# RWKV's 64x64 products on four quadrants of the array, with one pool of six PSUM banks

## The chip, the core and the metric

The kernel runs on one core of a Trainium2 chip. The time is the device time of one execution in microseconds, from a median of three runs. The engines are TensorE (PE, with its weight loads shown as PEld), VectorE (DVE), ScalarE (ACT), GpSimd (POOL) and SyncE (SP), which issues most DMAs. Matrix products are written to PSUM, which has eight banks of 128 partitions by 512 fp32 values.

## The reference

Two sequences of 1024 tokens with 1024 channels go through two layers, and then a norm. In each layer the normed input is multiplied with `w_in`, four mixers of 256 channels work on parts of the result, and their gated outputs are multiplied with `w_out` and added to the input.

```python
def _trunk(x, p):
    for l in range(DEPTH):
        zz = _rmsnorm(x, p['norm_g'][l]) @ p['w_in'][l]
        oA = _rwkv_mixer(zz[..., :A_W], ...)          # 4 heads of 64, two directions
        oB = _global_attn_mixer(...)                  # all keys, rotary
        oC = _rglru_mixer(...)
        oD = _window_attn_mixer(...)                  # |t - s| <= 128
        x = x + jnp.concatenate([oA, oB, oC, oD], -1) @ p['w_out'][l]
    return _rmsnorm(x, p['final_g'])

def step(S, inp):                                     # of mixer A, one token, both directions
    rt, wt, kt, vt, kkt, at = inp
    sk = jnp.einsum('bhij,bhj->bhi', S, kkt)
    S = S * wt[:, :, None, :] - sk[..., None] * (kkt * at)[:, :, None, :] + vt[..., None] * kt[:, :, None, :]
    return S, jnp.einsum('bhij,bhj->bhi', S, rt)
```

## The kernel before, in words

The work is cut into units, one for each layer and sequence. A front (`front`) norms a unit's input, makes the projections (`proj_store`, `proj_gate`, each 128 channels by 1024 tokens, three passes over high and low parts, in two tiles `pj` of PSUM), and runs mixers A and C. `mixer_bd` is attention for one or two units, `out_proj` and `out_last` the output projections. `ORDER` on line 38 gives the order in the program: F0 F1 B0 O0 F2 B1 O1 F3 B23 O23.

The program is written with tiles from pools. A planner lays down the order of each engine's instructions when the program is built: it goes through a simulated time, and on each engine takes the instruction that stands first in the program among those whose inputs are ready and for whose tile a buffer is free. On the chip each engine then follows that fixed order. So the projections of a front, which are written behind mixer A, and attention, which is written behind the next front or ahead of it, fill the time in which mixer A waits.

Mixer A (`mixer_a`) takes a pair of heads at a time, one on partitions 0-63 and one on 64-127, and half of the tokens, 8 chunks of 64: four blocks per front, 16 in all. For each block:

- `a_early` loads and shifts the inputs and normalizes the keys. `a_decay` makes the decays of a direction: two products `pl` of 512 columns, one from rows 0-63 of `up` and `wa` and one from rows 64-127, each followed by an activation that reads it.
- `a_prep_dir`, for each direction, multiplies the decayed keys `bk` and queries `ar` of each chunk and head: `pg` (192 columns, two chunks to a bank), then `pk` and `pn` (128 columns, four chunks to a bank). VectorE masks one part of each tile into `nl`, `kt`, `na`, and ScalarE copies the other.
- `tok` transposes the values of each chunk and head with the identity (64 columns, one bank, one ScalarE copy).
- `a_inverse` inverts the masked products by VectorE and by products of 32x32.
- `a_post`, for each direction and four chunks: `pf` (128 columns), a ScalarE copy into `xq`, then two `pw` (128 columns), each subtracted by VectorE from what it corrects. Then `pz` and `py`, products of 64 columns with the values.
- After two blocks `a_steps` runs the state through 16 chunks, one small product and one VectorE addition per step.

All these products are 64 by 64. In a bank the head on partitions 0-63 is computed from rows 0-63 of the array into its columns 0-63, the other head from rows 64-127 into columns 64-127, so two of the array's four quadrants are used. Both operands of a product lie on the partitions of its rows, and its result goes to the PSUM partitions of its columns.

PSUM's eight banks are divided by pools (lines 60 to 63): two for `pj`, three for `px` (attention's scores, rope, norms, transposes of the input and the output), two for `pa` (mixer A and the gates of mixer C), one for `ps` (`a_steps`, `a_out`).

Of the kernel before, what the change touches and what calls it, by code (L numbers as in the profile page):

```python
# [12 lines left out]
ALU = mybir.AluOpType  # L13
# [5 lines left out]
T = 1024  # L19
# [7 lines left out]
HC = NCH // 2  # L27
A_OFF, B_OFF, C_OFF, D_OFF = 0, 1152, 1920, 2432
# [23 lines left out]
class Trunk:  # L52
    def __init__(self, ctx, tc, w):
# [7 lines left out]
        self.pxp = pool("px", 3, space=PSUM)  # L61
        self.pap = pool("pa", 2, space=PSUM)
        self.psp = pool("ps", 1, space=PSUM)
# [3 lines left out]
    # ---- allocation helpers  # L67
# [33 lines left out]
    # ---- constants  # L101
# [39 lines left out]
    def load_layer(self, l):  # L141
# [39 lines left out]
        # softplus(-lam) = max(-lam, 0) + log1p(exp(-|lam|)), log1p(e) = 2 atanh(e / (2 + e))  # L181
# [28 lines left out]
    # ---- y = 1 / sqrt(x), x > 0, on small tiles  # L210
# [13 lines left out]
    # ---- 1/rms of each token, from the sums of squares over each partition's channels  # L224
# [20 lines left out]
    def x_first(self, pool, xs, xdram, st, hpool=None, L=None):  # L245
        """input tokens: 1/rms, channel-major to DRAM, normed if hpool is given"""
# [28 lines left out]
    def norm_rows(self, pool, st, half, ps):  # L275
        """st along the tokens, in every partition"""
# [74 lines left out]
    def proj_gate(self, pool, wsrc, c0, h, dst):  # L351
        """2 silu(gate), channel-major"""
# [52 lines left out]
        # unit keys  # L405
# [19 lines left out]
    def a_late(self, pool, keep, bd, L, P):  # L425
# [4 lines left out]
        # values, token-major by head, in place of the state's queries  # L430
# [5 lines left out]
        # bonus  # L436
# [6 lines left out]
    def a_decay(self, pool, d, L, P):  # L443
# [27 lines left out]
    def a_prep_dir(self, pool, keep, d, L, P):  # L471
        """decayed queries and keys of one direction, their products within the chunks, token-major forms"""
        nc = self.nc
        ch = lambda t: t.rearrange("p (c t) -> p c t", t=CH)
        H = [slice(0, 64), slice(64, 128)]
# [771 lines left out]
```

## Time and profile before

| what | value |
|---|---|
| time, median of three runs | 3475.95 us (3475.06 to 3481.63) |
| span of the profiled execution, first to last instruction | 3466.1 us |
| its own time | not given beyond the span; the median lies 9.85 us above the span |
| PE busy | 3180.8 us, 27314 products |
| DVE, ACT, POOL busy | 1931.1, 1283.9, 1160.0 us |
| mean granted clock of TensorE | 0.948 |

The busy time of an engine is the time in which at least one of its instructions runs; products that overlap count once. An fp32 product of the code appears in the profile as two products with two weight loads. A granted clock of 1.00 is 2.4 GHz, and 0.5 is 1.2 GHz.

### The profile page before, as it was taken

To read this page: it belongs to the slowest core of one execution; us is meant where nothing else is said; L and a number is where in the kernel's file an instruction comes from. 1 tells how busy PE (TensorE), PEld (TensorE's weight loads), DVE (VectorE), ACT (ScalarE), POOL (GpSimd) and SP (SyncE) were. 2 spreads that over 40 slices of the span, in tenths; PEclk is the share of its full clock that TensorE was granted. 3 is DMA by queue.
4 is the path that set the end of the run, shared out by engine and by line. 5 is a ranking of instruction groups with operands and counts; after the bars stand their busy time and mean duration, and the time that the engine had idled before them with its cause. 6 is when DMAs were issued, how large, how long until landed. Compare 5 with 4: busy or idle time off the path is not lost. (4 is left out here: it accounts for less than half of the span.)

```text
span 3466.1 us, 67345 instructions
## 1 busy us (share of the span) xinstructions
PE 3180.8 (92%) x27314; PEld 2253.7 (65%) x27314; DVE 1931.1 (56%) x3849; ACT 1283.9 (37%) x2397; POOL 1160.0 (33%) x1008
## 2 busy tenths in 40 slices
PE   6999999999779798999988989999999898898797
PEld 5777777777445476777666457777777554554486
DVE  6254434352886626423677957433663887679523
ACT  5332223222744423222544433324423434437322
POOL 2233232232432334222343333421333333434443
PEclk9999999999879899999989989999999898999799
DMA  7332333232220333323241124322333211111753
GB/s 247 107 109 83 92 115 92 91 90 91 91 76 16 114 117 127 89 80 94 90 149 51 39 80 145 120 85 83 125 112 99 63 38 54 49 46 38 260 190 133
DMA packets 382270, 343.99 MB, mean 99 GB/s; under 512 B 125708, under 2 KB 264968, under 8 KB 381960
## 3 DMA queue, kind: packets, MB, share of 16 engines
q1 hardware_dynamic: 242568, 270.48, 24.2%
q10 hardware_dynamic: 139392, 69.22, 7.1%
q8 instruction: 214, 3.51, 0.4%
q14 instruction: 96, 0.79, 0.1%
HBM read 217.84 MB, written 121.63 MB: 98 GB/s over the span
## 5 line engine op out<-in xcount | busy, mean ns | idle before, releaser
L99 PE MATMUL pj<-h,wh 128*128 128x512 f32 x3200 | 1063.3, 410 | 24.6 <-ACT h L234 11.1
L99 PEld LDWEIGHTS pj<-h,wh 128*128 128x128 f32 x3200 | 597.1, 190 | 213.0 <-issue 36.0
L324 POOL TENSOR_TENSOR wl<-wr,wh 128x512 fp32r<-128x512 f32 x264 | 354.1, 1341 | 1013.8 <-ACT wh L323 912.0
L99 PE MATMUL pj<-h,wl 128*128 128x512 f32 x1600 | 644.0, 407 | 1.9 <-POOL wl L324 1.9
L967 POOL TENSOR_TENSOR ac<-e,ac 128x512 f32<-128x512 f32 (+3 forms) x192 | 226.2, 1184 | 470.3 <-ACT e L954 309.0
L99 PE MATMUL pj<-oh,wh 128*128 128x512 f32 x1024 | 342.5, 414 | 34.0 <-ACT oh L234 23.9
L99 PE MATMUL px<-b,b 128*128 128x512 f32 (+6 forms) x1072 | 348.7, 415 | 27.0 <-DVE mxd L914 9.6
L99 PEld LDWEIGHTS pj<-h,wl 128*128 128x128 f32 x1600 | 304.2, 190 | 89.4 <-issue 19.9
L323 ACT CAST wh<-wr 128x512 fp32r<-128x512 f32 x264 | 163.2, 618 | 526.9 <-PE pj L99 517.1
L99 PEld LDWEIGHTS px<-b,b 128*128 128x128 f32 (+1 forms) x1072 | 191.0, 200 | 208.8 <-issue 139.9
L954 ACT ACTIVATE e<-px 128x512 f32<-128x512 f32 (+3 forms) x384 | 191.1, 516 | 246.2 <-PE px L99 238.6
L99 PEld LDWEIGHTS pj<-oh,wh 128*128 128x128 f32 x1024 | 195.9, 195 | 95.4 <-ACT oh L234 32.4
L99 PE MATMUL pa<-ar,bk 64*64 64x128 f32 (+1 forms) x2048 | 195.4, 314 | 27.2 <-ACT nl L507 13.7
L99 PE MATMUL pj<-oh,wl 128*128 128x512 f32 x512 | 204.5, 405 | 1.7 <-POOL wl L324 1.7
L97 PE MATMUL pj<-e,v 128*64 128x512 f32 (+3 forms) x768 | 186.9, 561 | 9.8 <-ACT e L954 9.5
L99 PEld LDWEIGHTS pa<-ar,bk 64*64 64x64 f32 x2048 | 132.3, 138 | 79.4 <-issue 37.5
L967 DVE TENSOR_TENSOR ac<-e,ac 128x512 f32<-128x512 f32 (+3 forms) x192 | 149.0, 780 | 54.3 <-ACT e L954 41.4
L626 DVE TENSOR_TENSOR kt<-kt,pa 128x512 f32<-128x512 f32 x64 | 43.8, 684 | 196.9 <-PE pa L99 196.7
L346 ACT ACTIVATE m<-pj 128x512 f32<-128x512 f32 x136 | 80.8, 594 | 134.2 <-PE pj L99 126.0
L99 PE MATMUL pa<-nl,bk 64*64 64x128 f32 x2048 | 126.3, 273 | 2.5 <-ACT bk L619 2.5
L99 PEld LDWEIGHTS pa<-nl,bk 64*64 64x64 f32 x2048 | 110.8, 133 | 26.0 <-issue 17.2
L902 DVE TENSOR_REDUCE mxb<-px 128x1 f32<-128x512 f32 x160 | 107.7, 682 | 35.5 <-PE px L99 34.9
(285 smaller groups left out, 5132.1 us busy)
## 6 DMA issues: line engine op xcount, KB each, us to landing
wr<-in_w_in_dram ACTq DMA_DIRECT2D x200, 256.0 KB
zd<-m SPq DMA_DIRECT2D x136, 256.0 KB
tg<-og SPq DMA_DIRECT2D x64, 512.0 KB
rw<-zd SPq DMA_DIRECT2D x192, 128.0 KB
og<-m SPq DMA_DIRECT2D x64, 256.0 KB
wr<-in_w_out_dram ACTq DMA_DIRECT2D x64, 256.0 KB
xo<-xd SPq DMA_DIRECT2D x64, 256.0 KB
halo<-zd SPq DMA_DIRECT2D x56, 256.5 KB
```

What stands on the lines that cost most here:

```text
L97: return self.nc.tensor.matmul(out=out, lhsT=lhsT, rhs=rhs, start=start, stop=stop, skip_group_check=True)
L99: self.nc.tensor.matmul(out=out, lhsT=lhsT, rhs=rhs, start=start, stop=stop)
L323: nc.scalar.copy(out=hi, in_=raw)
L324: nc.gpsimd.tensor_tensor(out=lo, in0=raw, in1=hi.bitcast(F32), op=ALU.subtract)
L346: self.nc.scalar.mul(out=m, in_=p, mul=scale)
L626: nc.vector.tensor_tensor(out=fl(dst), in0=fl(dst), in1=fl(pw), op=ALU.subtract)
L902: nc.vector.tensor_reduce(out=mx[:, i, half:half + 1], in_=p, axis=AX.X, op=ALU.max)
L954: last = nc.scalar.activation(out=e[:, :n], in_=p[:, :n], func=AF.Exp)
L967: (nc.gpsimd if (x + r) % ADDM else nc.vector).tensor_tensor(out=acc[r][:, os], in0=es[r][:, :n], in1=acc[r][:, os], op=ALU.add)
```

## The change

The three pools `px`, `pa` and `ps` become one pool of six banks, from which `px()`, `pa()` and `pss()` all take. `pj` keeps its two.

In mixer A the products of 64x64 outside `a_inverse`, `a_steps` and `a_out` are set out anew, over all four pairs of a row half and a column half (`QUADS`), in turn. Chunks 0-3 of a block go to one column half and chunks 4-7 to the other, and each of the two row halves has a bank of its own, so that the products of four (head, chunk) pairs follow each other with four different quadrants. The layout of `nl`, `kt`, `na`, `xq` follows: the index that was the chunk group is now the head, and the partition half is now the chunk group. In `a_post` the four quadrants carry the data back, so that `ar`, the state and `y` lie as before. The 192-column products of the second head are split in 64 and 128 columns, on different column halves. `tok` and `y` are copied by ScalarE in two pieces, since they now lie in two banks. In `a_decay` both tiles are taken and both products issued before the two activations. Comments are removed throughout.

```diff
+HS = (slice(0, 64), slice(64, 128))
+QUADS = ((0, 0), (1, 1), (1, 0), (0, 1))
-        self.pxp = pool("px", 3, space=PSUM)
-        self.pap = pool("pa", 2, space=PSUM)
-        self.psp = pool("ps", 1, space=PSUM)
+        self.pxp = pool("px", 6, space=PSUM)
...
     def pa(self, shape=(128, 512)):
-        return self.t(self.pap, "pa", shape)
+        return self.t(self.pxp, "px", shape)
     def pss(self, shape=(128, 512)):
-        return self.t(self.psp, "ps", shape)
+        return self.t(self.pxp, "px", shape)
...
     def tok(self, dst, src):
-        p = self.pa((128, HC, CH))
-        for j in range(HC):
-            for hs in (slice(0, 64), slice(64, 128)):
-                self.mm(p[hs, j], src(j)[hs], self.ident[hs, hs])
-        self.nc.scalar.copy(out=dst, in_=p)
+        ps = [self.pa((128, 4, CH)) for _ in range(2)]
+        for j in range(4):
+            for q, h in QUADS:
+                self.mm(ps[h][HS[q], j], src(4 * q + j)[HS[h]], self.ident[HS[h], HS[h]])
+        for h in range(2):
+            self.nc.scalar.copy(out=dst[:, 4 * h:4 * h + 4], in_=ps[h])
...
     def a_decay(...):
-        for (b0, dst, bias) in ((0, th, X_HW0), (64, tau, X_HA0)):
-            pl = self.pa()
-            self.mm(pl, L["up"][b0:b0 + 64, d, 128 * p:128 * p + 128], wa[b0:b0 + 64])
+        pls = [self.pa() for _ in range(2)]
+        for i in range(2):
+            self.mm(pls[i], L["up"][HS[i], d, 128 * p:128 * p + 128], wa[HS[i]])
+        for (pl, dst, bias) in ((pls[0], th, X_HW0), (pls[1], tau, X_HA0)):
             nc.scalar.activation(out=dst, in_=pl, func=AF.Tanh, scale=0.5, bias=...)
...
     def a_prep_dir(...):
-        for j0 in range(0, HC, 2):
-            pg = self.pa((128, 2, 3, CH))
+        for j0 in range(0, 4, 2):
+            pg = [self.pa((128, 2, 3, CH)) for _ in range(2)]
             for j in range(2):
-                for hs in H:
-                    self.mm(pg[hs, j], bk[hs, j0 + j], ar[hs, j0 + j])
+                c = [4 * q + j0 + j for q in range(2)]
+                self.mm(pg[0][HS[0], j], bk[HS[0], c[0]], ar[HS[0], c[0]])
+                self.mm(pg[1][HS[1], j, 0], bk[HS[1], c[1]], ar[HS[1], c[1], 0])
+                self.mm(pg[0][HS[1], j], bk[HS[0], c[1]], ar[HS[0], c[1]])
+                self.mm(pg[1][HS[0], j, 0], bk[HS[1], c[0]], ar[HS[1], c[0], 0])
+                self.mm(pg[1][HS[1], j, 1:3], bk[HS[1], c[0]], ar[HS[1], c[0], 1:3])
+                self.mm(pg[1][HS[0], j, 1:3], bk[HS[1], c[1]], ar[HS[1], c[1], 1:3])
...
-        for g in range(2):
-            pk, pn = self.pa((128, 4, 2, CH)), self.pa((128, 4, 2, CH))
-            for j in range(4):
-                c = 4 * g + j
-                for hs in H:
-                    self.mm(pk[hs, j], bk[hs, HC + c], ar[hs, c, 1:3])
-                    self.mm(pn[hs, j], ar[hs, c, 0], bk[hs, HC + c:2 * HC + 1:HC - c])
+        pk = [self.pa((128, 4, 2, CH)) for _ in range(2)]
+        for j in range(4):
+            for q, h in QUADS:
+                c = 4 * q + j
+                self.mm(pk[h][HS[q], j], bk[HS[h], HC + c], ar[HS[h], c, 1:3])
...
+        pn = [self.pa((128, 4, 2, CH)) for _ in range(2)]
+        for j in range(4):
+            for q, h in QUADS:
+                c = 4 * q + j
+                self.mm(pn[h][HS[q], j], ar[HS[h], c, 0], bk[HS[h], HC + c:2 * HC + 1:HC - c])
...
     def a_post(...):
-            for g in range(2):
-                pf = self.pa((128, 4, 2, CH))
-                for j in range(4):
-                    for hs in H:
-                        self.mm(pf[hs, j], nl[hs, 4 * g + j, 0], na[hs, j])
-                nc.scalar.copy(out=xq, in_=pf)
-                for (i, dst) in ((0, kt), (1, ar[:, 4 * g:4 * g + 4, 1:3])):
-                    pw = self.pa((128, 4, 2, CH))
-                    for j in range(4):
-                        for hs in H:
-                            self.mm(pw[hs, j], xq[hs, j, i], nl[hs, 4 * g + j, 1:3])
-                    nc.vector.tensor_tensor(out=fl(dst), in0=fl(dst), in1=fl(pw), op=ALU.subtract)
+            pf = [self.pa((128, 4, 2, CH)) for _ in range(2)]
+            for j in range(4):
+                for q, h in QUADS:
+                    self.mm(pf[h][HS[q ^ h], j], nl[HS[q], 4 * h + j, 0], na[h][HS[q], j])
+            for h in range(2):
+                nc.scalar.copy(out=xq[h], in_=pf[h])
+            pw = [self.pa((128, 4, 2, CH)) for _ in range(2)]
+            for j in range(4):
+                for q, h in QUADS:
+                    s = HS[q ^ h]
+                    self.mm(pw[h][HS[q], j], xq[h][s, j, 0], nl[s, 4 * h + j, 1:3])
+            for h in range(2):
+                nc.vector.tensor_tensor(out=fl(kt[h]), in0=fl(kt[h]), in1=fl(pw[h]), op=ALU.subtract)
...
+        pz = [self.pa((128, 2, 4, CH)) for _ in range(2)]
+        for d in range(2):
+            for j in range(4):
+                for q, h in QUADS:
+                    self.mm(pz[q][HS[h], d, j], P["kt", d, h][HS[q], j, 1], vt[HS[q], 4 * h + j])
...
+        for q in range(2):
+            nc.scalar.copy(out=y[:, 4 * q:4 * q + 4], in_=py[q])
```

The second `pw` (onto `ar`) and `py` are set out in the same way. The number of products stays, but for `pg`: 24 instead of 16 per direction and block.

## Rows read from the trace of the kernel before

**Rows 1.** The page: busy us of each engine (share of the span), x instructions
```profile
PE 3180.8 (92%) x27314; PEld 2253.7 (65%) x27314; DVE 1931.1 (56%) x3849; ACT 1283.9 (37%) x2397; POOL 1160.0 (33%) x1008
```
**Rows 2.** Table by windows, A beside projections: length, busy us, PEclk, DMA share, GB/s
```profile
480.00:840.00 360.00, 360.00 (x3162) 276.62 (x3161) 129.40 (x321) 92.64 (x181) 100.02 (x85) 1.00 0.29 87
...
sum 1645.00, PE 1621.09 PEld 1232.70 DVE 697.54 ACT 513.78 POOL 501.18; mean PE 270.18 PEld 205.45 DVE 116.26 ACT 85.63 POOL 83.53
```
**Rows 3.** Table by windows, A beside attention (PE, PEld, DVE, ACT, POOL)
```profile
880.00:1160.00 280.00, 243.31 (x1965) 136.96 (x1963) 225.31 (x404) 142.87 (x269) 104.72 (x99) 0.87 0.17 52
...
sum 1040.00, PE 926.10 PEld 549.46 DVE 837.34 ACT 501.76 POOL 390.31; mean PE 308.70 PEld 183.15 DVE 279.11 ACT 167.25 POOL 130.10
```
**Rows 4.** Same windows, instructions on tile pa alone: projections' six, attention's three
```profile
sum 1645.00, PE 375.53 PEld 272.85 DVE 123.95 ACT 124.84; mean PE 62.59 PEld 45.47 DVE 20.66 ACT 20.81
...
sum 1040.00, PE 297.03 PEld 211.75 DVE 89.54 ACT 93.63; mean PE 99.01 PEld 70.58 DVE 29.85 ACT 31.21
```
**Rows 5.** Timeline of PE, 64x64 runs: start us, length us, engine, line, operation, tiles
```profile
254.08 1.09 PE L99 MATMUL pa<-na,nl 64*64 64x128 f32 x16
255.10 0.50 PE L99 MATMUL pj<-h,wh 128*128 128x512 f32 x1
...
300.46 2.08 PE L99 MATMUL pa<-ar,kt 64*64 64x64 f32 x64
...
542.91 0.87 PE L99 MATMUL pa<-ar,bk 64*64 64x192 f32 x8
...
560.64 1.15 PE L99 MATMUL pa<-ident,v 64*64 64x64 f32 x32
...
577.55 1.52 PE L99 MATMUL pa<-ar,bk 64*64 64x192 f32 x16
...
652.14 1.96 PE L99 MATMUL pa<-nl,bk 64*64 64x128 f32 x32
```
**Rows 6.** Timeline of PE and PEld: products of 512 columns of other shapes
```profile
561.72 1.12 PE L99 MATMUL pa<-wa,up 64*128 64x512 f32 x2
...
867.41 1.98 PE L99 MATMUL pa<-cxc,gw 128*128 128x512 f32 x4
...
1048.97 0.20 PEld L97 LDWEIGHTS pj<-e,v 128*64 128x64 f32 x4 [0.25 <-ACT e L954]
1048.97 1.08 PE L97 MATMUL pj<-e,v 128*64 128x512 f32 x4
```
**Rows 7.** Groups by form, PE: xcount | busy us, mean ns | idle us before, releasers
```profile
L99 PE MATMUL pa<-ar,bk 64*64 64x192 f32 x1024 | 108.9, 346 | 13.1 <-ACT nl L507 6.1 <-DVE bk L490 3.9 <-ACT z L638 2.7
...
L99 PE MATMUL pa<-ar,bk 64*64 64x128 f32 x1024 | 87.4, 282 | 14.1 <-ACT nl L507 7.6 <-ACT kt L520 6.4
...
L99 PE MATMUL pa<-wa,up 64*128 64x512 f32 x128 | 76.9, 690 | 6.0 <-DVE kk L421 3.1 <-ACT na L522 2.9
...
L99 PE MATMUL pa<-cxc,gw 128*128 128x512 f32 x128 | 68.9, 646 | 6.2 <-ACT ctg L764 5.3 <-issue 0.8
```
**Rows 8.** Groups: score products of attention, and what reads them
```profile
L99 PE MATMUL px<-b,b 128*128 128x512 f32 (+6 forms) x1072 | 348.7, 415 | 27.0 <-DVE mxd L914 9.6
...
L954 ACT ACTIVATE e<-px 128x512 f32<-128x512 f32 (+3 forms) x384 | 191.1, 516 | 246.2 <-PE px L99 238.6 <-DVE ac L967 2.2 <-PE pj L99 1.8
...
L902 DVE TENSOR_REDUCE mxb<-px 128x1 f32<-128x512 f32 x160 | 107.7, 682 | 35.5 <-PE px L99 34.9
...
L914 DVE TENSOR_REDUCE mxd<-px 128x1 f32<-128x384 f32 (+1 forms) x80 | 41.2, 523 | 17.8 <-PE px L99 17.3
```
**Rows 9.** Timeline, tiles pk and pn of one group: first products, last copy
```profile
549.16 0.43 PE L99 MATMUL pa<-ar,bk 64*64 64x128 f32 x4
...
551.91 0.37 ACT L522 COPY na<-pa 128x256 f32<-128x256 f32 x1
```
**Rows 10.** Timeline of ACT: the copy of a pf into xq
```profile
646.91 0.59 ACT L619 COPY bk<-pa 128x512 f32<-128x512 f32 x1 [6.38 <-PE pa L99]
```
**Rows 11.** Instructions on tile pa, all engines, in 40 slices of the span
```profile
busy tenths in 40 slices 0899999999499997999999999999399999993000
```

More of the change, by code (lines that the diff above doesn't have):

```diff
@@ L499, in a_prep_dir @@
         P["nl", d] = nl
-        for j0 in range(0, HC, 2):
-            pg = self.pa((128, 2, 3, CH))
+        for j0 in range(0, 4, 2):
+            pg = [self.pa((128, 2, 3, CH)) for _ in range(2)]
             for j in range(2):
-                for hs in H:
-                    self.mm(pg[hs, j], bk[hs, j0 + j], ar[hs, j0 + j])
-            nc.vector.tensor_tensor(out=fl(nl[:, j0:j0 + 2, 0:2]), in0=fl(pg[:, :, 0:2]), in1=m(d, 0, 2, 2),
-                                    op=ALU.mult)
-            nc.scalar.copy(out=nl[:, j0:j0 + 2, 2], in_=pg[:, :, 2])
@@ new lines, in a_prep_dir @@
+                self.mm(pg[0][HS[0], j], bk[HS[0], c[0]], ar[HS[0], c[0]])
[5 more added lines that the diff above has]
+            for h in range(2):
+                n = slice(4 * h + j0, 4 * h + j0 + 2)
+                nc.vector.tensor_tensor(out=fl(nl[:, n, 0:2]), in0=fl(pg[h][:, :, 0:2]), in1=m(d, 0, 2, 2), op=ALU.mult)
+                nc.scalar.copy(out=nl[:, n, 2], in_=pg[h][:, :, 2])
@@ new lines, in a_prep_dir @@
+        for h in range(2):
+            P["kt", d, h] = self.t(pool, f"kt{d}{h}", (128, 4, 2, CH))
+            P["na", d, h] = self.t(pool, f"na{d}{h}", (128, 4, 2, CH))
+        pk = [self.pa((128, 4, 2, CH)) for _ in range(2)]
[3 more added lines that the diff above has]
+                self.mm(pk[h][HS[q], j], bk[HS[h], HC + c], ar[HS[h], c, 1:3])
+        for h in range(2):
+            kt = P["kt", d, h]
+            nc.vector.tensor_tensor(out=kt[:, :, 0], in0=pk[h][:, :, 0], in1=m(d, 1, 4), op=ALU.mult)
+            nc.scalar.copy(out=kt[:, :, 1], in_=pk[h][:, :, 1])
@@ L523, in a_prep_dir @@
+        pn = [self.pa((128, 4, 2, CH)) for _ in range(2)]
[3 more added lines that the diff above has]
+                self.mm(pn[h][HS[q], j], ar[HS[h], c, 0], bk[HS[h], HC + c:2 * HC + 1:HC - c])
+        for h in range(2):
+            na = P["na", d, h]
+            nc.vector.tensor_tensor(out=na[:, :, 0], in0=pn[h][:, :, 0], in1=m(1 - d, 0, 4), op=ALU.mult)
+            nc.scalar.copy(out=na[:, :, 1], in_=pn[h][:, :, 1])
         return kd
@@ L606, in a_post @@
         nc = self.nc
-        H = [slice(0, 64), slice(64, 128)]
+        fl = lambda t: t.rearrange("p n x t -> p n (x t)")
         for d in range(2):
@@ new lines, in a_post @@
+            na, kt = [[P[n, d, h] for h in range(2)] for n in ("na", "kt")]
+            pf = [self.pa((128, 4, 2, CH)) for _ in range(2)]
+            for j in range(4):
+                for q, h in QUADS:
+                    self.mm(pf[h][HS[q ^ h], j], nl[HS[q], 4 * h + j, 0], na[h][HS[q], j])
+            for h in range(2):
+                nc.scalar.copy(out=xq[h], in_=pf[h])
[4 more added lines that the diff above has]
+                    self.mm(pw[h][HS[q], j], xq[h][s, j, 0], nl[s, 4 * h + j, 1:3])
@@ new lines, in a_post @@
+            for h in range(2):
+                nc.vector.tensor_tensor(out=fl(kt[h]), in0=fl(kt[h]), in1=fl(pw[h]), op=ALU.subtract)
+            pw = [self.pa((128, 4, 2, CH)) for _ in range(2)]
+            for j in range(4):
+                for q, h in QUADS:
+                    s = HS[q ^ h]
+                    self.mm(pw[q][HS[h], j], xq[h][s, j, 1], nl[s, 4 * h + j, 1:3])
+            for q in range(2):
+                am = ar[:, 4 * q:4 * q + 4, 1:3]
+                nc.vector.tensor_tensor(out=fl(am), in0=fl(am), in1=fl(pw[q]), op=ALU.subtract)
@@ L627, in a_post @@
         vt = P["vt"]
+        pz = [self.pa((128, 2, 4, CH)) for _ in range(2)]
         for d in range(2):
-            pz = self.pa((128, HC, CH))
-            for c in range(HC):
-                for hs in H:
-                    self.mm(pz[hs, c], P["kt", d, c // 4][hs, c % 4, 1], vt[hs, c])
-            for g in range(2):
-                c0 = HC * hf + 4 * g
-                if d == 0:
-                    nc.scalar.copy(out=S["z"][c0 // 4][:, :, 0], in_=pz[:, 4 * g:4 * g + 4])
-                else:
-                    nc.scalar.copy(out=S["z"][(12 - c0) // 4][:, ::-1, 1], in_=pz[:, 4 * g:4 * g + 4])
@@ L639, in a_post @@
-        py = self.pa((128, HC, CH))
+            for j in range(4):
+                for q, h in QUADS:
+                    self.mm(pz[q][HS[h], d, j], P["kt", d, h][HS[q], j, 1], vt[HS[q], 4 * h + j])
+        for q in range(2):
+            c0 = HC * hf + 4 * q
+            nc.scalar.copy(out=S["z"][c0 // 4][:, :, 0], in_=pz[q][:, 0])
+            nc.scalar.copy(out=S["z"][(12 - c0) // 4][:, ::-1, 1], in_=pz[q][:, 1])
+        py = [self.pa((128, 4, CH)) for _ in range(2)]
         for d in range(2):
-            for c in range(HC):
-                for hs in H:
-                    self.mm(py[hs, c], P["kt", d, c // 4][hs, c % 4, 0], vt[hs, c], start=d == 0 and c == 0,
-                            stop=d == 1, skip=True)
+            for j in range(4):
+                for q, h in QUADS:
+                    self.mm(py[q][HS[h], j], P["kt", d, h][HS[q], j, 0], vt[HS[q], 4 * h + j],
+                            start=d == 0 and j == 0, stop=d == 1, skip=True)
@@ L645, in a_post @@
         y = P["ar", 1][:, :, 0]
-        nc.scalar.copy(out=y, in_=py)
+        for q in range(2):
+            nc.scalar.copy(out=y[:, 4 * q:4 * q + 4], in_=py[q])
         S["y", hf] = y
```

12 lines of the change are left out of this document (1 added, 11 removed).

## The prediction

> **What bounds the kernel now.** I read the page's busy table first [rows 1]: TensorE is busy 3180.8 us of 3466.1 (92%), VectorE 56%, ScalarE 37%, so no other engine comes near over the whole run. Such a share hides stages, and the table by windows came next. In six windows where mixer A runs beside the projections, TensorE is busy 1621 of 1645 us, at a granted clock of 1.00 in the one shown, and VectorE only 698 [rows 2]. There every microsecond taken off TensorE comes off the path, because the next projection stands right behind in its queue. In three windows where mixer A runs beside attention, TensorE is busy 926 of 1040 us, at a clock of 0.87 in the one shown, and VectorE 837 [rows 3]: two engines near their limit, and TensorE time is worth less. Instructions on the tile `pa`, nearly all of them mixer A's, hold 375.5 us of TensorE in the six windows and 297.0 in the three [rows 4]: 56% and 44%.
>
> Then the question how fast 64x64 products run today. One product in the code is two records (the 8 products of one `pf` are 16 records). Two timeline runs of one shape and different length give the pace without their ends: 16 more records cost 1.96 - 1.09 = 0.87 us at 128 columns, 32 more cost 2.08 - 1.15 = 0.93 at 64 columns, 8 more cost 1.52 - 0.87 = 0.65 at 192 [rows 5]. Per two records that is 109, 58 and 163 ns. The two records are the two heads': the code puts them on the diagonal of the array, (rows 0-63, columns 0-63) and (rows 64-127, columns 64-127).
>
> **The quadrants.** Each of 16 blocks (4 fronts, 4 half pairs) has, by the code, 32 products of 192 columns, 160 of 128 (per direction 16 each in `pk`, `pn`, `pf`, 32 in `pw`) and 80 of 64 (16 in `tok`, 32 each in `pz`, `py`). A pair of products takes two pair steps, so there are as many steps as products: 32 x 163 + 160 x 109 + 80 x 58 = 27.3 us per block, 437 us in all. After the change four products stand in four quadrants. For 128 and 64 columns that halves the steps. The 192-column products of the second head are split in 64 + 128: a group of four costs its longest quadrant, 2 x (58 + 109) = 334 ns, eight groups per block, 2.7 us for 5.2. After: 2.7 + 8.7 + 2.3 = 13.7 us per block. Saved: 13.6 x 16 = 218 us.
>
> Do four run at once? The value products of two heads share all 128 rows and differ in columns: four records of 512 columns take 1.08 us, while four of `gw`, each on the whole array and so one by one, take 1.98 [rows 6]. So two column halves fed from the same rows run side by side, as the two row halves do above. What no row shows is two row halves writing the same 64 PSUM partitions at once, as (0,0) and (1,0) now do, each in a bank of its own. Bounds: 0 to 218. I take 90%, 196 us, since a quad falls back to pairs where the planner finds the second of its two banks taken.
>
> The four weight loads of those value products are over within 0.20 us, while the products on the same rows go on to 1.08 [rows 6]. The Trainium skill (TensorE: Matmul & The Clock Gate, "Part 3: Packing small matmuls") says that a weight load overlaps running matmuls only where its row group differs, which speaks against two quadrants on the same rows; the rows above differ from it, and it stays as a rival.
>
> **The decays.** `a_decay` made two products of 512 columns with an activation between them; now both are issued together, and they sit on the two row halves. One takes 1.12 us; side by side two should take what the value pair takes, 1.08 us [rows 6]. 32 x (2 x 1.12 - 1.08) = 37 us. Bounds 0 (the planner still puts projections between) to 37.
>
> **Changes of shape.** A run of 16 records holds the engine from 254.08 to 255.10, 1.02 us for 8 steps of 0.109 [rows 5]: 0.15 us per run to get in and out of 64x64. Per direction and block the runs go from 10 to 12 (4 `pg`, 2 `pk` with `pn`, 2 `pf`, 2 to 4 `pw`) to 7. 32 x 3 to 5 x 0.15 = 14 to 24 us. Since broken quads make new runs I take 12; bounds 0 to 24.
>
> **The banks.** Mixer A (with C's gates) had two banks, its state steps one, attention and rope three; now all share six. TensorE's idle time just ahead of the four costliest waits on `pa` is 39 us (13.1 + 14.1 + 6.0 + 6.2) [rows 7], ahead of the score products on `px` 27 us [rows 8]. All of it gone would be 66 us; I take a third, 22. Downwards: a score tile may now wait for a bank in A's hands. There are 624 score tiles on `px` (384 + 160 + 80) [rows 8]; the length of one eviction, 0.37 us [rows 9], for each would be -231 us. The value lies near the idle rows, as A's bursts are short: the two tiles of `pk` and `pn` are made and read within 3.1 us (549.16 to 552.28) [rows 9].
>
> **What else moves.** VectorE's evictions keep number and size. ScalarE copies `tok` and `y` in two pieces: 32 more copies, 2 x 0.37 [rows 9] for 0.59 us [rows 10], 5 us on an engine busy 37%, hidden behind projections, and 5 us if not. No DMA is added or moved, so SP's and POOL's queues keep their order but for the planner's new timing. The one wait added is on the first product that writes a quad's second bank: behind it in TensorE's order stand that quad's other products and whatever the planner put next, and VectorE and ScalarE wait for those with their evictions.
>
> **The sum.** In the six windows a saved microsecond counts full, in the three attention windows I count 0.6 (between 0, if VectorE takes over, and 1; TensorE at 89% is nearer to the upper end): 0.56 + 0.44 x 0.6 = 0.82. Quadrants 196 x 0.82 = 162, decays 37 x 0.82 = 30, shapes 12, banks 22: 226 us. Span 3466.1 - 226 = 3240. The median of the runs shown is 3475.95, 9.85 above the span of the one profiled; no other time of that execution is given, so I add 9.85: 3250 us, 6.5% faster. Its own range is 3210 to 3300.
>
> **Rivals.**
> 1. VectorE takes over beside attention, and nothing of the 44% is gained. For: 837 of 1040 us busy there, and the granted clock, already 0.87, would fall further where TensorE idles more [rows 3]. Against: TensorE's 89% in the same rows. 0.56 x (196 + 37) + 12 = 142, banks nothing: 3334 us.
> 2. A's chain was the spine. `pa` has work in nearly every slice [rows 11], and between a ScalarE copy that ends at 647.50 [rows 10] and the products that read it, at 652.14 [rows 5], lie 4.6 us. With six banks the planner can close such gaps, and A's next unit starts earlier. Against: TensorE is full beside the projections anyway. All of quadrants, decays, shapes and idle rows: 196 + 37 + 24 + 66 = 323, 3153 us.
> 3. Two row halves on the same PSUM partitions take turns, so quads are no faster than pairs. 30 + 12 + 22 = 64: 3412 us.
> 4. Weight loads wait for products on the same rows. A 128-column step of four then takes 109 + 58 = 167 for 218, a 64-column one 116 for 116 (no gain), a group of 192 columns 334 + 4 x 58 = 566 for 650 (27% of its saving). 47% of the 140 us of 128 columns plus 27% of 40: 77, x 0.9 x 0.82 = 57, and 64: 121, 3355 us.
> 5. Slower: the score tiles starve. Attention loses its three own banks to A's bursts of two to six. It decides from 226 / 624 = 0.36 us of wait per score tile; at 0.5 us, 312 us, the time is 3562 us. For: ScalarE already waits 238.6 us for score products [rows 8]. Against: six banks stand where three were, and A's are free again in about 3 us.
>
> **How the numbers follow.** Forecast 0.50, rival 1 0.17, 2 0.12, 3 0.08, 4 0.07, 5 0.06. The range 3140 to 3400 holds the forecast and rivals 1, 2 and 4, about 0.83 with their tails. Only rival 5 is slower, and a mild form of it could end within 0.2%, about the least that a measurement here can tell from no change: faster 0.92, same 0.03, slower 0.05.
>
> **What would show it.** Right: four records start close together and the next four 109 ns later at 128 columns, so that the 16 records of a `pf` that took 1.09 us take about 0.6; TensorE's busy time near 2950 us at a share of about 91%; the two products of `a_decay` as one run of four records. Wrong: fours that go as two pairs 109 ns apart (rivals 3 and 4, by where the weight loads start); attention windows as long as before with VectorE above 85% (rival 1); ScalarE's wait for score products well above 238.6 us (rival 5). A time under 3200 or above 3300 would mean that a term above is mis-sized by more than its working allows.

## The result and the profile after

The changed kernel takes 3852.58 us (median of 4 runs) beside 3475.51 for the kernel before: ratio 1.1078, 95% interval 1.1062 to 1.1094. The forecast was 3250, the range 3140 to 3400. It is 10.8% slower, and the direction was wrong.

The page of the kernel after: busy us and share of each engine; TensorE's busy tenths in 40 slices; the granted clock, likewise.
```profile
PE 3045.1 (79%) x27826; PEld 2201.8 (57%) x27826; DVE 1912.3 (50%) x3849; ACT 1284.9 (33%) x2429; POOL 1141.9 (30%) x1008
...
PE   7999844899965487999997448798989744788998
...
PEclk9999865899975688989997668898999855889999
```
TensorE is busy 136 us less than in [rows 1], and its share falls from 92% to 79%. The slices show four holes (44, 54, 44, 44) that the kernel before does not have, and the granted clock falls in each. Mean clock and span of the kernel after:
```profile
core 0: 3851.1 us, clock 0.852
```
Between the two levels 2.4 and 1.2 GHz, 0.852 means (1 - 0.852) x 2 x 3851 = 1140 us at the lower one; before, at a mean of 0.948, it was 360 us of 3466.

The table by windows of the kernel after names the holes (length; busy us of PE, PEld, DVE, ACT, POOL; clock; DMA share; GB/s). First, mixer A beside projections:
```profile
710.00:1110.00 400.00, 372.65 (x3987) 289.01 (x3988) 172.91 (x397) 127.76 (x258) 97.74 (x95) 0.96 0.31 92
...
sum 1510.00, PE 1402.98 PEld 1087.46 DVE 662.11 ACT 475.98 POOL 363.20; mean PE 350.74 PEld 271.87 DVE 165.53 ACT 119.00 POOL 90.80
```
Second, A's end, C and rope with no projections beside them, a kind of stretch that did not exist before:
```profile
1110.00:1320.00 210.00, 107.79 (x1805) 81.64 (x1805) 103.61 (x242) 61.12 (x99) 37.47 (x33) 0.62 0.11 33
...
sum 880.00, PE 451.33 PEld 340.32 DVE 432.37 ACT 254.82 POOL 160.85; mean PE 112.83 PEld 85.08 DVE 108.09 ACT 63.70 POOL 40.21
```
Third, attention, now without A:
```profile
1330.00:1510.00 180.00, 156.82 (x640) 86.61 (x640) 127.73 (x196) 81.48 (x165) 83.74 (x71) 0.89 0.15 47
...
sum 725.00, PE 619.02 PEld 338.53 DVE 534.63 ACT 332.27 POOL 345.67; mean PE 206.34 PEld 112.84 DVE 178.21 ACT 110.76 POOL 115.22
```
In the 880 us of the second kind no engine is busy more than 51%, and the clock is 0.62 in the one shown. Before, those stages lay beside projections and attention [rows 2, 3].

The products did get faster. The timeline of PE after (start us, length us, records):
```profile
404.50 1.12 PE L99 MATMUL px<-bk,ar 64*64 64x128 f32 x32
...
406.03 1.13 PE L99 MATMUL px<-wa,up 64*128 64x512 f32 x4
...
467.36 1.99 PE L99 MATMUL px<-na,nl 64*64 64x128 f32 x32 [0.75 <-DVE nl L620]
```
Against [rows 5], 32 records of 128 columns take 1.12 us for 1.96: four quadrants run side by side, two row halves onto the same PSUM partitions among them. Against [rows 6], four decay records take 1.13 us, where two took 1.12. The third row shows the clock eating the gain: in a hole, at 1.2 GHz (granted clock 0.50 from 467 to 470 us), a quad run of 32 takes 1.99 us, as long as the pairs took before.

What grew is waiting. Instructions on rope's tile `rp`, by windows, of the kernel before and then after:
```profile
170.00:400.00 230.00, 15.85 (x84) 11.52 (x84) 8.24 (x12) 3.79 (x6) 22.85 (x18) 1.00 0.33 99
...
570.00:710.00 140.00, 6.24 (x36) 4.73 (x36) 2.75 (x4) 2.52 (x4) 7.25 (x6) 1.00 0.29 88
```
```profile
170.00:400.00 230.00, 0.00 (x0) 0.00 (x0) 0.00 (x0) 1.27 (x2) 0.00 (x0) 0.98 0.29 84
400.00:570.00 170.00, 0.00 (x0) 0.00 (x0) 0.00 (x0) 0.00 (x0) 0.00 (x0) 0.74 0.19 50
570.00:710.00 140.00, 28.81 (x84) 18.67 (x84) 23.56 (x28) 3.69 (x6) 23.33 (x18) 0.61 0.21 70
```
Before the change all 84 products of the front's six ropes had run by 400 us. After it two of rope's activations had run by 400 us, so its input was there, and not one product until 570. The timeline of PE after shows what they stood behind:
```profile
573.69 3.78 PE L99 MATMUL px<-ident,ar 64*64 64x64 f32 x64 [6.73 <-DVE gnt L219]
577.39 1.86 PE L99 MATMUL px<-bones,rp 128*128 128x2 f32 x8
```
The first row is the last products of mixer A (`a_out`), the second rope's first, right behind them. TensorE had sat idle for 6.73 us, until VectorE released A's products, and ran no product of rope in that time.

And the next front stood behind rope. Instructions on `rp`, first of the kernel before, then of the kernel after: kind, count, shortest/median/longest ns, first and last start.
```profile
L99 PE MATMUL px<-bones,rp x192: 165/251/272, 202.7 to 2566.1; 128*128 128x2 f32 x192
...
L305 DVE SCALAR_TENSOR_TENSOR m<-m,par,rp x48: 733/748/1893, 443.4 to 2253.4; 128x512 f32<-128x512 f32 x48
```
```profile
L99 PE MATMUL px<-bones,rp x192: 209/352/374, 577.4 to 3238.8; 128*128 128x2 f32 x192
...
L305 DVE SCALAR_TENSOR_TENSOR m<-m,par,rp x48: 739/751/1771, 682.2 to 2637.5; 128x512 f32<-128x512 f32 x48
```
L305 is the norm that opens the next front, at 682.2 us for 443.4. Its first step, a ScalarE copy into `rp` at 678.9, waits 11.5 us for rope's last addition on GpSimd: by the code, rope works in the front's SBUF space, which the next front takes over. So behind the first front there was no next projection to fill TensorE for some 240 us. In the other three holes it is attention that comes late: its first products on `px` start at 1337.5 us, after the second hole, and at 879.3 before the change.

The theory that the runs test: **a pool gives its banks out in the order of the program, so in one shared pool a tile written later in the program waits until every earlier one has its bank.** Rope, C's gates and attention are all written behind mixer A. (The planner, as described ahead of the prediction, takes any ready instruction "for whose tile a buffer is free"; by the theory a bank is free only for the tile whose turn it is.) The rival: six banks for all are too few, whatever the order. The expectations below name two more: quads need two banks at once and lose them to others ("starving"), and the quadrants' products spoil the planned order ("planner").

### The profile page after: what moved, and what is told of

It is laid out like the page before. It is cut to its first block, busy times and chain, and to the rows that moved or that the text cites. A ratio compares the mean times of both kernels' runs of the same rounds, so it can differ in the third digit from the quotient of the medians.

```text
span 3851.1 us, 68791 instructions
## 1 busy us (share of the span) xinstructions
PE 3045.1 (79%) x27826; PEld 2201.8 (57%) x27826; DVE 1912.3 (50%) x3849; ACT 1284.9 (33%) x2429; POOL 1141.9 (30%) x1008
## 5 line engine op out<-in xcount | busy, mean ns | idle before, releaser
L99 PE MATMUL px<-b,b 128*128 128x512 f32 (+6 forms) x1072 | 319.4, 405 | 1.1 <-ACT e L980 0.6
L99 PEld LDWEIGHTS px<-b,b 128*128 128x128 f32 (+1 forms) x1072 | 206.8, 208 | 124.5 <-issue 88.7
L993 DVE TENSOR_TENSOR ac<-e,ac 128x512 f32<-128x512 f32 (+3 forms) x192 | 180.3, 955 | 63.1 <-POOL ac L993 33.0
L1079 DVE TENSOR_TENSOR xo<-xo,pj 128x512 f32<-128x512 f32 x64 | 44.0, 687 | 218.8 <-PE pj L99 218.7
L833 PE MATMUL px<-ident,rp 128*128 128x128 f32 x96 | 26.8, 434 | 130.0 <-POOL rp L828 130.0
L687 DVE TENSOR_TENSOR z<-z,px 128x128 f32<-128x128 f32 x112 | 32.0, 285 | 195.0 <-PE px L99 195.0
L99 PE MATMUL px<-ar,bk 64*64 64x128 f32 (+2 forms) x2560 | 99.9, 295 | 34.2 <-DVE bk L495 31.9
L645 DVE TENSOR_TENSOR kt<-kt,px 128x512 f32<-128x512 f32 x64 | 41.9, 685 | 171.0 <-PE px L99 171.0
L99 PE MATMUL pj<-b,b 128*128 128x512 f32 (+1 forms) x144 | 69.6, 483 | 69.9 <-DVE mxb L928 33.2
L99 PE MATMUL px<-bk,nl 32*32 32x16 f32 (+1 forms) x3072 | 42.3, 197 | 93.6 <-ACT bk L577 81.4
```

Of the source, the lines that this page charges most:

```text
L99: self.nc.tensor.matmul(out=out, lhsT=lhsT, rhs=rhs, start=start, stop=stop)
L645: nc.vector.tensor_tensor(out=fl(kt[h]), in0=fl(kt[h]), in1=fl(pw[h]), op=ALU.subtract)
L687: nc.vector.tensor_tensor(out=z(i), in0=z(i), in1=zp, op=ALU.add)
L833: nc.tensor.transpose(out=pb[:, 128 * i:128 * i + 128], in_=ex[:, 128 * i:128 * i + 128], identity=self.ident)
L993: (nc.gpsimd if (x + r) % ADDM else nc.vector).tensor_tensor(out=acc[r][:, os], in0=es[r][:, :n], in1=acc[r][:, os], op=ALU.add)
L1079: nc.vector.tensor_tensor(out=xo, in0=xo, in1=p, op=ALU.add)
```

## The experiments

All ratios are to the kernel before, with 95% intervals. In the diffs `+` is the experiment; `-` is the changed kernel, or the kernel before where the text says so.

**The two halves of the change apart.** Quadrants with the old pools:
```
-        self.pxp = pool("px", 6, space=PSUM)
+        self.pxp = pool("px", 3, space=PSUM)
+        self.pap = pool("pa", 2, space=PSUM)
+        self.psp = pool("ps", 1, space=PSUM)
...
-        return self.t(self.pxp, "px", shape)
+        return self.t(self.pap, "pa", shape)
...
-        return self.t(self.pxp, "px", shape)
+        return self.t(self.psp, "ps", shape)
```


> The changed kernel with the three pools of before put back (px 3 banks, pa 2, ps 1). Order theory (a pool hands its banks out in the order in which the program asks, so in one pool everything written behind mixer A waits until A took its last bank): the loss is gone and the quadrants' gain stays, 3200 to 3300 us; the first rope product runs beside mixer A again, at about 250 us into the span, not after 580. Starving theory (quads need two banks at once and lose them to others): with two banks for A it gets worse, over 3500. Planner theory (the quadrants' products themselves spoil the planned order): still 3700 to 3900.

Measured 3410.97 us, 0.9801 (0.9770 to 0.9831). The loss is gone, which the starving and the planner theory do not allow, but the time lies 111 us above the range of the order theory. And the kernel before, with nothing but the one pool:
```
-        self.pxp = pool("px", 3, space=PSUM)
-        self.pap = pool("pa", 2, space=PSUM)
-        self.psp = pool("ps", 1, space=PSUM)
+        self.pxp = pool("px", 6, space=PSUM)
...
-        return self.t(self.pap, "pa", shape)
+        return self.t(self.pxp, "px", shape)
...
-        return self.t(self.psp, "ps", shape)
+        return self.t(self.pxp, "px", shape)
```


> The kernel before with nothing changed but its three pools merged into one of six banks. Order theory: slower than the changed kernel or near it, 3900 to 4050 us, with rope after mixer A and TensorE idle for some 700 us or more. Starving theory: 3450 to 3550, since pairs of products need one bank at a time. Planner theory: 3475 plus or minus 40.

Measured 4069.91 us, 1.1697 (1.1663 to 1.1732). So the pool alone costs 4070 - 3476 = 594 us, and the rest of the change gives 4070 - 3853 = 217 on top of it, 65 with the old pools. The whole loss is the pool's; the starving and planner theories, which expected at most 3550 here, fall.

**Two pools instead of one or three** (`px` 3; `pa`, `ps` and the gates share 3):
```
-        self.pxp = pool("px", 6, space=PSUM)
+        self.pxp = pool("px", 3, space=PSUM)
+        self.pap = pool("pa", 3, space=PSUM)
...
-        return self.t(self.pxp, "px", shape)
+        return self.t(self.pap, "pa", shape)
...
-        return self.t(self.pxp, "px", shape)
+        return self.t(self.pap, "pa", shape)
```


> The changed kernel with two pools: px 3 banks, and one of three for mixer A's blocks, its state steps and C's gates. Order theory: rope and attention are free of A, 3250 to 3400 us; C's gates and the next pair's blocks still stand behind A's state steps, so it is slower than with three pools. Starving theory: like three pools or better, as A has three banks for two. Planner theory: 3700 to 3900.

Measured 3444.18 us, 0.9917 (0.9887 to 0.9947), 44 us above the range. Sharing among instructions that are all mixer A's and C's costs 33 us beside the three pools: fewer pools alone are not the trouble.

**One late tile in attention's pool.** The kernel before, where only the state steps move into `px`, which gets their bank:
```
-        self.pxp = pool("px", 3, space=PSUM)
+        self.pxp = pool("px", 4, space=PSUM)
...
-        self.psp = pool("ps", 1, space=PSUM)
...
-        return self.t(self.psp, "ps", shape)
+        return self.t(self.pxp, "px", shape)
```


> The kernel before, without quadrants; only the one bank of the state steps (ps) joins px, which then has four; pa keeps its two. Order theory: that alone is enough, since rope and attention now stand behind the state steps that end mixer A: 3850 to 4100 us, first rope product after the first unit's last step (above 900 us if A goes at its old pace, 600 if A runs alone). Shortage theory: faster or same, 3430 to 3480, as no one has fewer banks.

Measured 4112.56 us, 1.1834 (1.1816 to 1.1853), the slowest of all and 13 us above the range. Instructions on `rp` of that kernel:
```profile
L98 PE MATMUL px<-bones,rp x192: 209/352/372, 676.6 to 3494.7; 128*128 128x2 f32 x192
...
L304 DVE SCALAR_TENSOR_TENSOR m<-m,par,rp x48: 737/751/1768, 745.4 to 2828.0; 128x512 f32<-128x512 f32 x48
```
Mixer A kept its two banks, and no bank was lost to anyone. But the state steps, A's last work, now stand ahead of rope in `px`, and rope begins at 676.6 instead of 202.7, the norm at 745.4 instead of 443.4.

**Rope out of the shared pool** (the changed kernel, `px` 5, one bank for rope):
```
-        self.pxp = pool("px", 6, space=PSUM)
+        self.pxp = pool("px", 5, space=PSUM)
+        self.prp = pool("pr", 1, space=PSUM)
...
-        pst = self.px((128, 4, 2))
+        pst = self.pr((128, 4, 2))
...
-        pb = self.px()
+        pb = self.pr()
...
-        pp = self.px()
+        pp = self.pr()
```


> The changed kernel, but rope's three tiles per step come from a pool of their own of one bank, and the shared pool has five. Order theory: rope runs beside mixer A again (from about 250 us), so the front's input is free early and the next front's norm and projections start before mixer A ends, at 400 to 550 us instead of 682; C's gates and attention still stand behind A. Between the changed kernel and three pools: 3550 to 3750 us. If a shortage of banks were the cause: no better than 3850, as A and attention have one bank less.

Measured 3629.48 us, 1.0454 (1.0430 to 1.0477). Rope's products begin at 211.9 us, the time drops by 223 with one bank less in the pool, and what is left is attention. Instructions on its tile `b` in three windows:
```profile
940.00:980.00 40.00, 4.00 (x7) 2.14 (x7) 2.76 (x4) 9.56 (x16) 12.35 (x10) 0.75 0.49 146
980.00:1200.00 220.00, 0.00 (x0) 0.00 (x0) 0.00 (x0) 0.00 (x0) 0.00 (x0) 0.65 0.12 30
1200.00:1390.00 190.00, 90.84 (x297) 56.90 (x297) 6.78 (x4) 18.61 (x32) 12.12 (x10) 0.87 0.09 31
```
Its inputs are there and 7 products run, all into the projections' tile `pj`; then none for 220 us, while the next front's A and C finish (A's last output at 1173 us, C's scans from 1189), and then all, from 1208 us.

**C's gates moved.** Quadrants with the three old pools, the gates from `px` instead of `pa` (two lines against that version):
```
-                            pg = self.pa()
+                            pg = self.px()
```


> Three pools as before, the quadrants, and the gates of mixer C taken from px instead of pa. Order theory: in pa the gates stand behind the whole of A, in px they don't, so mixer C's scans come out while A still runs (before the last state steps of A); time 3180 to 3290, at or under quads with three pools. Starving theory: no difference to three pools beyond 1%. Planner theory: 3700 to 3900.

Measured 3856.03 us, 1.1084 (1.1054 to 1.1113): a miss, 566 us above the range, and as slow as the whole change. (It lies in the range of the planner theory, which the 3411 us with the same quadrants had excluded.) I had not asked what is written behind the gates in `px`. C's SBUF space lies over mixer A's, so the gates come after A's blocks (the last products that read `xq` end at 593 us, the gates run from 603.6 to 642.2), and what is written behind them in `px` waits with them: the first front's last two ropes start at 643 us, its first four, which are written ahead of the gates, had run by 305. One late tile in attention's pool is enough. From `ps` instead:
```
-                            pg = self.pa()
+                            pg = self.pss()
```


> Quadrants with the three pools of the kernel before, C's gates moved from mixer A's two banks to the one bank of the state steps. Theory (order decides, and both pools' instructions ahead of the gates are mixer A's): no change by more than 1%, 3380 to 3440 us. Rival (the gates in two banks side by side hold C back): over 3450 us.

Measured 3556.49 us, 1.0250 (1.0222 to 1.0279): a miss again, 145 us above 3411. The products on `gw` from 500 to 1100 us, first with the gates in `pa`, then in `ps`:
```profile
L101 PE MATMUL pa<-cxc,gw x32: 590/592/1057, 806.6 to 843.7; 128*128 128x512 f32 x32
```
```profile
L101 PE MATMUL ps<-cxc,gw x32: 590/592/1223, 867.9 to 927.8; 128*128 128x512 f32 x32
```
In `pa` the gates pass A's last state steps; in `ps` they stand behind them (those products run until 842 us). They also take 60 us there for 37, in one bank for two; what each of the two costs, the runs do not divide.

**How many banks attention needs.** Quadrants with two banks for attention and three for A; in the second run `pa` has four and the state steps are in it:
```
-        self.pxp = pool("px", 6, space=PSUM)
+        self.pxp = pool("px", 2, space=PSUM)
+        self.pap = pool("pa", 3, space=PSUM)
+        self.psp = pool("ps", 1, space=PSUM)
...
```


> Quadrants with separate pools, one bank moved from px to pa: px 2, pa 3, ps 1. If the rest of the quadrants' gain in the three-pool version is lost to A's two banks (a quad needs both at once, so pn waits for pk's eviction): the products of bk and ar fall from 61 and 86 us of TensorE to about 45 and 65, the decays from 65 to below 55, and the time to 3350 to 3400 us. If attention needs its three banks: 3420 to 3480.

> Quadrants with two pools: px 2 banks, and 4 for mixer A, its state steps and C's gates. Order theory: as with px 3 and 4 minus 1 (3444 us) A is apart from rope and attention, but the gates stand behind the state steps; more banks give full quads. If full quads count for more than the steps' place in the order: 3330 to 3400 us; if not, or if attention needs its third bank, 3420 to 3500.

Measured 3578.36 (1.0295; 1.0271 to 1.0320) and 3547.64 (1.0199; 1.0174 to 1.0224), both above every range named. The control, the kernel before with the same banks:
```
-        self.pxp = pool("px", 3, space=PSUM)
-        self.pap = pool("pa", 2, space=PSUM)
+        self.pxp = pool("px", 2, space=PSUM)
+        self.pap = pool("pa", 3, space=PSUM)
```


> The kernel before, with attention and rope on two banks, mixer A with C's gates on three, the state steps on one; no quadrants. Theory (a bank taken from attention costs whatever mixer A does): 3600 to 3660 us, as the version with quadrants lost 167 us by the same move, and in the windows with attention the score products wait longer. Rival (the loss came from the quadrants with three banks, which put A's bursts ahead of attention): 3450 to 3500 us.

Measured 3653.94 us, 1.0521 (1.0491 to 1.0551). Taking attention's third bank for A costs 181 us without quadrants and 167 with them. The group that reads its score tiles in that kernel:
```profile
L954 ACT ACTIVATE e<-px 128x512 f32<-128x512 f32 (+3 forms) x384 | 193.1, 515 | 316.1 <-PE px L99 313.5 <-POOL ac L967 0.2
```
313.5 us of waits for score products, 238.6 with three banks [rows 8].

**What TensorE's time is worth.** The kernel before, with `pk`, `pn` and `pw` issued twice (work that the reference does not have):
```
-                    self.mm(pk[hs, j], bk[hs, HC + c], ar[hs, c, 1:3])
+                    for _ in range(2):
+                        self.mm(pk[hs, j], bk[hs, HC + c], ar[hs, c, 1:3])
...
```


> The kernel before, with every product of pk, pn and pw issued twice into the same place. By the pace of the trace that is 16 blocks x (32 x 163 + 32 x 109 + 64 x 109 ns), bounded between 224 us (pk, pn and pw at 109 ns a pair) and 251 us of added TensorE work. If TensorE's time is worth 0.82 of itself, as the forecast took, 3660 to 3690 us. If TensorE's time is worth little because other waits take it up (rival), 3520 to 3600 us.

Measured 3704.16 us, 1.0661 (1.0641 to 1.0681), 14 us above the range: 231 us more. The page shows what was added:
```profile
PE 3432.9 (93%) x31410; PEld 2517.2 (68%) x31410; DVE 1922.9 (52%) x3849; ACT 1284.9 (35%) x2397; POOL 1163.4 (31%) x1008
```
TensorE is busy 252 us more than in [rows 1], so added work costs 0.92 of its length.

**The decays alone** (quadrants, old pools, `a_decay` as before):
```
-        pls = [self.pa() for _ in range(2)]
...
+        for (b0, dst, bias) in ((0, th, X_HW0), (64, tau, X_HA0)):
+            pl = self.pa()
+            self.mm(pl, L["up"][b0:b0 + 64, d, 128 * p:128 * p + 128], wa[b0:b0 + 64])
```


> Quadrants with the three pools of the kernel before, but the two products of a_decay one after the other, each with its activation, as before. If the pair of decays side by side is worth its 30 us with two banks: 3435 to 3450 us. If taking both banks of mixer A at once costs what the pair saves (rival): 3390 to 3415 us.

Measured 3412.15 us, 0.9818 (0.9798 to 0.9839), the same as 3411: with two banks the pair brings nothing. With six it brings nothing either: the kernel before with the one pool, its decays in the old order, has
```profile
L97 PE MATMUL px<-wa,up 64*128 64x512 f32 x128 | 38.0, 672 | 0.0
```
38.0 us for the 76.9 of [rows 7], and the changed kernel 36.4. The decays became shorter by the banks, not by their new order.

**Order alone.** Two runs keep the changed kernel's pool of six and change only the order of the program. Rope, and the C, B and D projections, between A's half pairs (`mixer_a` yields after its first one):
```
-                k.mixer_a(keep, zd, L, od[0:2])
+                mixa = k.mixer_a(keep, zd, L, od[0:2])
+                next(mixa)
...
+                for _ in rope:
+                    pass
+                for _ in mixa:
+                    pass
```


> The changed kernel with its one pool of six banks, and nothing but the order in the program changed: C's, B's and D's projections and rope stand between the two half pairs of mixer A, where they stood behind both. Theory (the shared pool gives its banks out in the order of the program, so rope waits for A's last bank): rope ends before 500 us where it began at 587, the next front's norm begins between 420 and 560 where it began at 682, attention stays behind the next A, and the time is 3500 to 3750 us. Rival (six banks are too few for all, whatever the order): rope and norm where they were within 50 us, 3800 to 3900 us.

Measured 3836.54 us, 1.1041 (1.1018 to 1.1063). Tile `rp`, then tile `b` by windows:
```profile
L99 PE MATMUL px<-bones,rp x192: 167/251/372, 403.7 to 3021.7; 128*128 128x2 f32 x192
...
L305 DVE SCALAR_TENSOR_TENSOR m<-m,par,rp x48: 719/748/1716, 478.5 to 2613.5; 128x512 f32<-128x512 f32 x48
```
```profile
1090.00:1130.00 40.00, 3.66 (x6) 1.76 (x6) 2.76 (x4) 9.58 (x16) 13.10 (x10) 0.63 0.49 145
1130.00:1300.00 170.00, 0.56 (x1) 0.33 (x1) 0.00 (x0) 0.00 (x0) 0.00 (x0) 0.68 0.12 28
1300.00:1490.00 190.00, 91.09 (x297) 57.70 (x297) 4.08 (x4) 18.54 (x32) 12.67 (x10) 0.87 0.09 31
```
Rope came at 403.7 us, right behind the first half pair, and the norm at 478.5, as the theory had it and the rival did not; attention stopped after 6 products, all into `pj`, until A and C were through. The time was a miss (3500 to 3750 expected) and lies in the rival's range, so here the starts decide and not the time: A's second half pair now stood behind the projections and rope (its steps from 670 us, 544 in the changed kernel), so a wait only changed owners. Attention ahead of the next front:
```
-ORDER = "F0 F1 B0 O0 F2 B1 O1 F3 B23 O23"
+ORDER = "F0 B0 F1 O0 B1 F2 O1 F3 B23 O23"
```


> The changed kernel with its one pool, and the first two attention units written ahead of the next front in the program, where they stood behind it; nothing else. Theory (order of the program): the first unit's attention begins before 1000 us where it began at 1349, the next front's mixer A waits for attention's last bank, the two still run one after the other, and the time is 3650 to 4000 us. Rival (attention's score tiles lose the banks to A's bursts, whatever the order): attention begins no earlier than 1200 us.

Measured 3861.08 us, 1.1112 (1.1088 to 1.1135). Tile `b` by windows:
```profile
680.00:870.00 190.00, 93.84 (x304) 58.61 (x304) 7.09 (x8) 28.09 (x48) 24.92 (x20) 0.89 0.17 54
870.00:1340.00 470.00, 0.00 (x0) 0.00 (x0) 0.00 (x0) 0.00 (x0) 0.00 (x0) 0.92 0.30 89
```
Attention's first products on `px` start at 692 us instead of 1338; the next front's A starts behind it, its first decay products at 923 instead of 739. In these runs the order decides who waits, and with one pool somebody always did.

## Why the prediction was wrong

**The step that failed is "The banks".** It says "now all share six", puts idle rows of 66 us on one side and one eviction of 0.37 us per score tile on the other, and takes +22. Measured by the pool alone it is -594. The price was asked of the wrong thing: I counted how long a bank is held (3 us), when the question was whose turn it is. I let a free bank go to the first instruction that is ready; what the runs show is that it goes to the next tile in the program, and a tile that is not ready keeps all behind it waiting. The old pools were not a matter of number but three separate queues, which let rope run beside A, and attention beside the next A. Two locks follow: rope behind A, and with it the next front's norm (682 for 443 us); attention behind the next A and C. Rope apart takes off 223 us (3853 to 3629); the 218 from there to 3411 is attention's lock with what the moved banks cost, which the runs do not divide.

**"What else moves" failed with it.** "The one wait added is on the first product that writes a quad's second bank": the waits that mattered were of instructions that the diff does not touch.

**"The quadrants" and "Changes of shape" held as work of TensorE; "The decays" did not.** Inside the shared pool the 64x64 products of the change hold TensorE for 264 us in the changed kernel and 474 with the pool alone (counted from the traces' records, time at 1.2 GHz by half): 210 less, where 196 + 12 were forecast. Four quadrants run at once at the pace that was worked out: in the run at 404.50 a new group of four records starts every 0.109 us. The two decay products do take 1.13 us for 1.08, but that came with the banks, as shown above. That the time falls by 217 us, beside a forecast of 162 + 30 + 12 = 204, is luck in part: 30 of it were the decays, and the weight of 0.82 was worked out for a kernel whose TensorE is hardly ever idle. The 9.85 us added to the span are of little weight and too much: in the later runs of the kernel before the time is 2 us above its own span.

**With the old pools 65 us are left, and there the weight in "The sum" failed too.** Counted as above, TensorE has 3045 us of work before and 2901 with quadrants and the old pools: 143 less, of 196 + 37 + 12 = 245 forecast without the weight. The other half of the time at 1.2 GHz rises by 72 us (136 to 208) and idle time by 16, so the span falls by 56 (3466.1 to 3410.5): 0.39 of the work saved, not 0.82. That work added in the kernel before costs 0.92 of itself does not carry over to work taken away.

Two things are shown. First, less work is saved: with two banks a quad holds both, and the groups of PE there are these (before: 126.3, 85.8 and 76.9 us for `nl,bk`, `bk,ar` and `wa,up`):
```profile
L101 PE MATMUL pa<-nl,bk 64*64 64x128 f32 x2048 | 99.6, 278 | 9.4 <-ACT bk L640 5.2 <-DVE kt L647 4.1
L101 PE MATMUL pa<-wa,up 64*128 64x512 f32 x128 | 68.1, 715 | 0.6 <-ACT ar L395 0.6
L101 PE MATMUL pa<-bk,ar 64*64 64x128 f32 x1024 | 64.0, 308 | 11.3 <-ACT kt L533 11.1
```
In the changed kernel `bk,ar` is at 54.5 and `wa,up` at 36.4. Second, the clock: beside attention, by windows of that kernel,
```profile
860.00:1150.00 290.00, 254.11 (x2086) 140.29 (x2086) 227.59 (x442) 125.39 (x262) 103.07 (x101) 0.80 0.17 48
```
0.80 for the 0.87 of [rows 3], TensorE busy no shorter (254 us of 290 for 243 of 280) and VectorE as long (228 for 225). Of 158 us more at 1.2 GHz in the whole run, some 130 lie in the three stretches with attention. A's last output in the first front comes 61 us earlier than before (893 for 954), the end of the first attention 27 (1142 for 1169), that of the second 10 (2039 for 2048). So beside attention little is gained, as rival 1 had it, but its sign, VectorE above 85%, did not come (78%). What the trace shows is the clock; why it is lower there at the same busy share stays open.

**The account of the 385 us of span.** TensorE's busy time, at 1.2 GHz counted half: 3045 before, 2724 after, -321. Some 110 of it come with the pool alone, which with the old products has 2935: 34 are the decays, 36 the other 64x64 products, the rest is not divided. The other half of the time at 1.2 GHz: 136 to 321, +185. Idle between the first product and the last: 256 to 778, +522. Together +386.

**The rivals.** 2 seems half right, since A does run much faster (last output of the first front at 578 us for 954), but not for its reason: with A's old two banks and no quadrants, where only the state steps moved into `px`, that output comes at 677 us. So 277 of the 376 us come without banks or quadrants for A, when the projections no longer run beside it. 3 and 4 fell: 32 records of 128 columns, a quarter of them on each quadrant, go in 1.12 us, so neither PSUM partitions nor weight loads on the same rows hold them up. That differs from the rule of the Trainium skill (TensorE: Matmul & The Clock Gate, "Part 3: Packing small matmuls") that a weight load overlaps running matmuls only where its row group differs. The 3411 us with the old pools lie beside rival 3's 3412 by chance. 5 had the sign and 0.06 of the chance, but not the mechanism: score tiles were to starve between A's bursts, and ScalarE's wait for them above 238.6 us was to show it. Its row after says less waiting, because attention now runs alone:
```profile
L980 ACT ACTIVATE e<-px 128x512 f32<-128x512 f32 (+3 forms) x384 | 185.3, 518 | 149.9 <-PE px L99 133.8 <-POOL ac L993 6.0 <-PE pj L97 3.2
```
Of the signs named ahead, "TensorE's busy time near 2950 us at a share of about 91%" was the one that told: 3045 at 79%.

The best version is the quadrants with the three old pools: 3411 us, 2.0% under the kernel before and 11.5% under the change (3411 / 3853).

## What to carry to other kernels

In a program like this one a pool of buffers is a queue in the order of the program, so before two pools are merged, ask of each tile which earlier tiles come due later than it; one late tile (C's gates, or the state steps) in the pool of an early one cost 445 and 637 us here, without a bank less for anyone. Work taken off the bound engine pays in full only where other work fills its place: with the old pools 143 us less of it gave 56, as the clock took back 72 and idle time 16. And a change in two parts is run in two parts first: here one was worth -65 and the other +594.

## What the hardware showed that was not expected

Two products in different row halves of the array write the same 64 PSUM partitions at once, each in its own bank, at full pace (32 records of 128 columns in 1.12 us for 1.96 [rows 5]). A stretch at half clock takes back what a shape gains: 1.99 us for the same 32 records at a granted clock of 0.50, in a window (440 to 680 us) where TensorE is busy 124 of 240 us.
